# An encoder layer in one launch: the second embedding sum moved behind the fourth tile, and another order for the last two products and the final norm

## Chip, cores and metric

The kernel runs on one core of a Trainium2 chip. The metric is the device time of one execution in microseconds (us). Six kinds of queue matter below: TensorE (PE in the profile, with its weight loads as PEld), VectorE (DVE), ScalarE (ACT), GpSimd (POOL), SyncE (SP, which here only issues loads and stores), and the DMA engines that all these transfers share.

## The reference

One layer of a bidirectional encoder over a sequence of 1024 tokens of width 1024, all in float32. The parts before the first norm (retention, windowed attention, output projection) are not touched by the change. What follows is this:

```python
h = _layer_norm(ALPHA * h + mix, ln1_gain[i], ln1_bias[i])
g = h @ w_ffn_gate[i]
up = h @ w_ffn_up[i]                                # hidden width 2816
ffn = (jax.nn.silu(g) * up) @ w_ffn_down[i]
ple = p[i] @ w_ple_proj[i]                          # p: 1024 x 256
ple_gate = jax.nn.sigmoid(h @ w_ple_gate[i])        # 1024 x 1024 weight
h = _layer_norm(ALPHA * h + ffn + ple_gate * ple, ln2_gain[i], ln2_bias[i])
```

`_layer_norm(x, g, b)` is `(x - mean) * rsqrt(var + 1e-5) * g + b` over the 1024 columns of a row.

## The kernel before, in words

**Arithmetic.** Every float32 operand of a large product is split in two: a high part, copied by ScalarE (L71), and the low part that is left, subtracted by VectorE (L72). A product of 128x128 by 128x512 is then three matmuls (high by high, high by low, low by high; `mm3` at L77 to L79, `mm3c` at L763 to L765). The large matrix products are not made in four quadrant products of a 2x2 block scheme with eight terms but by a seven-product scheme (Strassen's kind): sums and differences of blocks are multiplied, and each of the products 1 to 7 is added to or subtracted from one or more quadrants of the result. Outputs of 128x512 are accumulated in eight PSUM banks, in four pairs with the tags `mm`, `s`, `t`, `o`.

**Stages.** Retention and attention run until about 370 us, the output projection and the first norm until about 470 us, then the gate of the per-layer embedding, the gate and up projections (about 555 to 870 us), the down projection, and the second norm.

**Order.** Inside a manual scope the order of the instructions on an engine is the order of the program; outside it a scheduler chooses the order from its own estimates. One scope holds TensorE and SyncE from early on. A second scope, `es3`, holds VectorE, ScalarE and GpSimd until `es3.close()`, which stands in the embedding stage. The whole down projection is in a scope that holds all five engines. SyncE's loads and stores go out in the order of its queue, each waiting for its data; GpSimd issues the accumulating DMAs, which add a tile in memory to one that is already in place.

**The embedding stage** (from about 470 us). `t_sums` (L995 to L1038) gives a list of steps that make the left operands of products 5, 6, 7 and 4, called sums 1 to 4, from blocks of the normed h: `both` takes three VectorE passes for a sum, `less` takes two (L1011, L1012; the third sum's are at L1004 to L1006), each over 128x1024, and `put` splits it (L71, L72). A sum has two halves, q = 0 and 1. Ahead of product 5 stand four tiles that finish a quadrant: for each, TensorE makes 12 matmuls into a bank, then `first_tile` calls `embed` (L1051 to L1062): four to six matmuls for p @ W_pe into another bank, the sigmoid on ScalarE, the product of both on VectorE (L1059, which frees that bank), and an addition into the tile's accumulator (L1060). Steps of the second sum are put between these tiles in VectorE's order: the half 0 of the second sum behind the second and third tile, half 1 and half 0 of the third sum ahead of product 5, the rest of the third sum inside product 5, the fourth sum inside product 6. Each of the products 5, 6, 7 and 4 is 48 matmuls into four banks; its results are added to others on VectorE (L1072 and `add4`).

**The down projection.** The 2816 hidden columns are cut in eleven pairs of blocks, and these in two segments of five and six (`SEG`). A unit is one product of one block pair: `dload` brings the blocks (and, for some, an accumulating DMA on GpSimd's queue makes their sum, L1340), `dprep` splits them, `dmm` does the matmuls (four row tiles, three matmuls each), and after a product's last unit `dpost` adds the four banks to the accumulators `acc`. There are 77 units; `d_step` does one and loads and splits ahead. The last two products are number 7 of the second segment (72 matmuls), which is subtracted from the right halves of tiles 0 to 3 (L1398), and number 4 (72 matmuls), which is added to the left halves (L1396, with the row sums; tile 3's at L1398). Tiles 4 to 7 are complete some time before that, since product 3 finishes them.

**The second norm.** For tiles 4 to 7 (`ln2_steps`) it is: squares with their sum on ScalarE (L1413), two scalar steps on VectorE and two on GpSimd (L1408 to L1449), one scaling pass on ScalarE over 1024 columns (L1452), one multiplication by the gain on VectorE, and an accumulating DMA that adds the bias (L1456). The list `later` spreads these steps over the units of the last products, and their stores (L1512) go out on SyncE ahead of those of tiles 0 to 3. For tiles 0 to 3 (`tail`) it is four VectorE passes over 512 columns: two for the mean and the gain (`center`, L1434), two for the deviation and the bias (`scale`, L1440), with no DMA but the stores; tile 3, `LAST`, takes its statistics by BATCH_NORM_STATS2 on VectorE (L1400).

Of the kernel before, what the change touches and what calls it, by code (L numbers as in the profile page):

```python
# [12 lines left out]
ALU = mybir.AluOpType  # L13
# [29 lines left out]
def layer(tc, xT, xn, w_first, w_mt, w_rv, w_out, w_pg, w_pe, pT, w_gu, w_dn,  # L43
# [951 lines left out]
    def t_sums():  # L995
# [21 lines left out]
        def step(n, q, parts=(0, 1)):  # L1017
# [19 lines left out]
            [lambda k=k: step(2, 0, (k,)) for k in range(2)] + \  # L1037
            [lambda n=n, q=q: step(n, q) for n, q in ((2, 1), (3, 0), (3, 1), (4, 0), (4, 1))]  # L1038
# [61 lines left out]
    for k in range(4):  # L1100
# [19 lines left out]
    product(6, Y, True, TT[2], steps[7:9])  # L1120
# [250 lines left out]
    def dmm(p, n, k, ts, first, stop):  # L1371

        a, b = dops[p, n]
        for t in ts:
            c = slice(t * P, (t + 1) * P)
            mm3c(dbank[k][t], a[:, 0, c], a[:, 1, c], b[:, 0, :], b[:, 1, :], first, stop)

    hs = [slice(h * HF, (h + 1) * HF) for h in range(2)]
    accd, R, later = [], [], []
# [12 lines left out]
    def addto(t, h, b, op=ALU.add, done=False):  # L1392
# [6 lines left out]
        if done and t == LAST:  # L1399
            dve.bn_stats(stts[t][:, 6 * h:6 * h + 6], half(t, h))  # L1400
        elif done:
            act.activation(ct([P, HF], "sg", 2), half(t, h), AF.Copy, accum_out=stts[t][:, h:h + 1])

    LAST = 3

# [9 lines left out]
    def var(t):  # L1415

        stt = stts[t]
        if t == LAST:
            dve.bn_aggr(stt[:, 12:14], stt[:, 0:12])
            dve.tensor_scalar(stt[:, 12:13], stt[:, 12:13], -1.0, None, ALU.mult)  # L1420
        else:
            negmean(t)
            squares(t)

    def rstd(t):
        stt = stts[t]
        if t != LAST:
            dve.tensor_scalar(stt[:, 13:14], stt[:, 2:3], stt[:, 3:4], 1.0 / D, ALU.add, ALU.mult)
# [3 lines left out]
    def center(t):  # L1432
        for h in range(2):
            x = half(t, h)  # L1434
            dve.scalar_tensor_tensor(x, x, stts[t][:, 12:13], ln2[0][:, hs[h]], ALU.add, ALU.mult)

    def scale(t):
        for h in range(2):
            x = half(t, h)
            dve.scalar_tensor_tensor(x, x, stts[t][:, 15:16], ln2[1][:, hs[h]], ALU.mult, ALU.add)  # L1440
            sp.dma_start(out[t][:, hs[h]], x)

    def ln2_steps(t):
# [7 lines left out]
        def second():  # L1451
            act.activation(x, x, AF.Identity, bias=stt[:, 11:12], scale=stt[:, 15:16])  # L1452

        def third():
            dve.tensor_tensor(x, x, ln2[0], ALU.mult)
            pool.dma_start(x, ln2[1], accum_op=ALU.add)  # L1456
# [249 lines left out]
```

## Time and profile before

| | |
|---|---|
| median of three runs | 1199.84 us (1199.11 to 1200.37) |
| the profiled execution | 1199.99 us |
| its span (first to last instruction) | 1198.0 us |
| granted TensorE clock, mean | 0.998 of full speed |
| last matmul begins | 1188.70 us |
| last store issued | 1195.04 us |

All times in the views are counted from the span's start. A row of the timeline gives start, duration, engine, line, operation, tiles written and read, shape, and how many of them; in brackets the wait ahead of it and what ended it. A row of the waits gives the engine, the operation that waited, what released it, then the total, the count and the longest. A row of the windows gives the stretch, its length, the busy time with the number of instructions of TensorE, its weight loads, VectorE, ScalarE and GpSimd, then SyncE's, the granted clock, the mean busy share of the DMA engines and what they moved in GB/s.

### The profile page before, as it was taken

How to read it: one execution, taken by the hardware profiler on the slowest of the kernel's cores; microseconds unless marked ns; L12 is line 12 of the kernel's file. 1: busy time of each engine (PE TensorE's matmuls, PEld its weight loads, DVE VectorE, ACT ScalarE, POOL GpSimd, SP SyncE). 2: the span in 40 equal slices, each digit the busy share in tenths (PEclk: the TensorE clock that was granted, in tenths of full speed). 3: DMA queues.
4: the chain of work that ended last, by engine and by line, in shares of the span. 5: the costliest groups of instructions: out<-in, count | busy, mean ns of one | idle time of the engine just before them, and what ended most of it. 6: DMA issues, size and time to landing. Idle time of an engine off the chain costs nothing.

```text
span 1198.0 us, 16664 instructions
## 1 busy us (share of the span) xinstructions
PE 1181.0 (99%) x5892; PEld 983.9 (82%) x5892; DVE 771.5 (64%) x1346; ACT 542.5 (45%) x1046; POOL 363.8 (30%) x342
## 2 busy tenths in 40 slices
PE   9999999999999999999999999999999999999996
PEld 7888888888888888788888888888888888888885
DVE  5654788877767788947744555545554565775668
ACT  5566238676786257203323332333322325562463
POOL 2001020202010022002756465555746342034232
PEclk9999999999999999999999999999999999999999
DMA  6335635434336864666233311332123169999977
GB/s 251 110 136 211 250 120 212 160 123 162 121 126 232 324 232 167 237 219 211 88 123 132 130 64 71 132 132 98 78 88 132 71 202 300 355 276 207 263 182 210
DMA packets 78098, 207.80 MB, mean 173 GB/s; under 512 B 9024, under 2 KB 13248, under 8 KB 78016
## 3 DMA queue, kind: packets, MB, share of 16 engines
q1 hardware_dynamic: 69376, 189.98, 44.0%
q0 software_dynamic: 8640, 16.78, 8.0%
q8 instruction: 46, 0.75, 0.2%
q14 instruction: 36, 0.29, 0.1%
HBM read 139.35 MB, written 62.13 MB: 168 GB/s over the span
## 4 chain that ended last, share of the span: by engine, by line
PE 94%; DVE 3%; ACT 1%; issue 1%; DMA 0%; POOL 0%; DVEq 0%; SPq 0%; ACTq 0%
PE bmm L77 6%; PE bt L763 6%; PE bt L764 6%; PE bt L765 6%; PE bmm L79 6%; PE bmm L78 6%; PE bs L763 6%; PE bs L764 6%; PE bs L765 6%; PE bo L763 5%; PE bo L764 5%; PE bo L765 5%; PE bmm L764 5%; PE bmm L763 5%; PE bmm L765 5%; PE bo L553 2%
## 5 line engine op out<-in xcount | busy, mean ns | idle before, releaser
L77 PE MATMUL bmm<-H,w 128*128 128x512 f32 x240 | 96.8, 403 | 0.4 <-ACT H L71 0.4
L79 PE MATMUL bmm<-H,w 128*128 128x512 f32 x240 | 94.1, 392 | 0.0
L78 PE MATMUL bmm<-H,w 128*128 128x512 f32 x240 | 93.8, 391 | 0.0
L1168 POOL TENSOR_TENSOR H<-ln 128x512 f32<-128x512 f32 x22 | 29.2, 1327 | 180.9 <-DMA ln<-in_w_gu 174.3
L1198 POOL TENSOR_TENSOR ev<-ev 128x512 f32<-128x512 f32 x33 | 54.9, 1664 | 91.2 <-DVE ev L1213 64.2
L72 DVE TENSOR_TENSOR w<-H,w 128x512 fp32r<-128x512 f32 x44 | 39.1, 889 | 63.1 <-ACT w L71 63.1
L72 DVE TENSOR_TENSOR w<-raw,w 128x512 fp32r<-128x512 f32 x56 | 45.3, 810 | 45.7 <-ACT w L71 45.2
L514 POOL COPY sc<-skb 128x1 f32<-128x1 f32 x64 | 13.0, 208 | 188.3 <-PE bt L541 149.4
L1196 ACT ACTIVATE ev<-ev 128x512 f32<-128x512 f32 x33 | 20.9, 632 | 103.5 <-DVE ev L1213 103.5
L1202 POOL TENSOR_TENSOR ev<-ev,ev 128x512 f32<-128x512 f32 x44 | 62.7, 1436 | 2.6
L72 DVE TENSOR_TENSOR u<-H,u 128x512 fp32r<-128x512 f32 x47 | 37.1, 790 | 38.9 <-ACT u L71 38.6
L77 PEld LDWEIGHTS bmm<-H,w 128*128 128x128 f32 x240 | 45.2, 188 | 10.5 <-ACT H L71 1.3
L79 PEld LDWEIGHTS bmm<-H,w 128*128 128x128 f32 x240 | 45.0, 188 | 10.0
L78 PEld LDWEIGHTS bmm<-H,w 128*128 128x128 f32 x240 | 45.1, 188 | 7.7
L71 ACT ACTIVATE u<-H 128x512 fp32r<-128x512 f32 x47 | 29.7, 631 | 43.5 <-PE bt L765 9.0
L523 ACT ACTIVATE sc<-sc,st 128x385 f32<-128x385 f32 (+1 forms) x64 | 37.2, 584 | 25.3 <-DVE st L521 25.2
L519 DVE CUSTOM_DVE_ANT_0 sc<-cst,bs,skb 128x384 f32<-128x384 f32 (+1 forms) x64 | 34.9, 576 | 16.3 <-PE bs L518 15.7
L71 ACT ACTIVATE w<-raw 128x512 fp32r<-128x512 f32 x56 | 34.7, 624 | 17.1 <-PE bo L79 7.0
L475 POOL TENSOR_TENSOR sm<-sm,cst 128x8 f32<-128x8 f32 x8 | 15.6, 1950 | 86.9 <-DVE sm L474 86.9
L874 POOL TENSOR_TENSOR stt<-stt,cst 128x1 f32<-128x1 f32 x8 | 12.1, 1514 | 91.2 <-DVE stt L873 91.2
L1172 POOL TENSOR_TENSOR H<-raw,H 128x512 f32<-128x512 f32 x22 | 37.8, 1718 | 0.0
L71 ACT ACTIVATE w<-H 128x512 fp32r<-128x512 f32 x44 | 27.4, 622 | 21.4 <-PE bs L765 6.3
(802 smaller groups left out, 3822.6 us busy)
## 6 DMA issues: line engine op xcount, KB each, us to landing
ad<-ev SPq DMA_DIRECT2D x33, 512.0 KB, 2.7
pgd<-pro SPq DMA_DIRECT2D x28, 512.0 KB, 2.8
raw<-in_w_gu SPq DMA_DIRECT2D x22, 512.0 KB, 4.3
ln<-in_w_gu SPq DMA_DIRECT2D x22, 512.0 KB, 3.5
raw<-ad SPq DMA_DIRECT2D x40, 256.0 KB, 5.5
ln<-ad SPq DMA_DIRECT2D x37, 256.0 KB, 6.7
H<-in_w_dn SPq DMA_DIRECT2D x33, 256.0 KB, 7.7
wod<-aq SPq DMA_DIRECT2D x15, 512.0 KB, 2.6
```

Of the source, the lines that this page charges most:

```text
L71: act.activation(hi, raw, AF.Copy)
L72: dve.tensor_tensor(lo, raw, hi.bitcast(F32), ALU.subtract)
L77: pe.matmul(o, lh, rh, start=start, stop=False)
L78: pe.matmul(o, lh, rl, start=False, stop=False)
L79: recent[0] = pe.matmul(o, ll, rh, start=False, stop=stop).ins.name
L523: act.activation(sc[g][:, :nk + 1], sc[g][:, :nk + 1], AF.Exp, bias=st_[:, 1, j, g:g + 1], accum_out=st_[:, 2, j, g:g + 1])
L763: pe.matmul(o, lh, rh, start=start, stop=False, skip_group_check=True)
L764: pe.matmul(o, lh, rl, start=False, stop=False, skip_group_check=True)
L765: pe.matmul(o, ll, rh, start=False, stop=stop, skip_group_check=True)
L1172: pool.tensor_tensor(s[3], a(0, 1), s[0], ALU.subtract)
L1198: pool.tensor_tensor(c[:, 1, :], c[:, 0, :], c[:, 1, :], ALU.mult)
L1202: pool.tensor_tensor(self.ev[dst][:, 0, :], left, right, op)
```

## The change

In the embedding stage, the second sum is no longer made between the four tiles: both of its halves stand behind the fourth tile, ahead of product 5. `es3.close()`, the end of the scope that holds VectorE, ScalarE and GpSimd to the program's order, moves from before product 5 to behind it.

At the end, of product 7's units for tiles 2 and 3 only the first two are done at its place; the other four, with the subtraction, are done between the tiles of product 4 (`rest`), which for these two tiles is then summed in a fresh bank, and the held bank is also added to the left half. Tiles 0 and 1 are as they were, and product 4 adds to their banks. The last tile is made in two halves of 256 columns, each with its own statistics, into a scratch tile `lst`. Tiles 0 to 2 are normed as tiles 4 to 7 are: one pass on ScalarE, one multiplication on VectorE, and an accumulating DMA for the bias (tile 2 in two halves of 512 columns). The steps of the norm of tiles 4 to 7 are spread further: fewer of them stand beside product 7, more between the tiles of product 4. SyncE's stores come in the order 4, 5, 6, 7, 0, 1, the first half of 2, the first half of 3, the second half of 2, and two quarters of 3.

```diff
@@ t_sums
         return [lambda k=k: [step(1, q, (k,)) for q in range(2)] for k in range(2)] + \
-            [lambda k=k: step(2, 0, (k,)) for k in range(2)] + \
-            [lambda n=n, q=q: step(n, q) for n, q in ((2, 1), (3, 0), (3, 1), (4, 0), (4, 1))]
+            [lambda n=n, q=q: step(n, q) for n in (2, 3, 4) for q in range(2)]
@@ the four tiles
-        if k in (1, 2):
-            steps[k]()
+        if k == 1:
+            steps[1]()
     gate_w(5, (2, 3))
     first_tile(3)
-    es3.close()
-    for k in range(3, 5):
+    for k in range(2, 4):
         steps[k]()
     gate_w(6)
     Z = four("b")
-    product(5, Z, True, TT[1], steps[5:7], True)
+    product(5, Z, True, TT[1], steps[4:6], True)
+    es3.close()
...
-    product(6, Y, True, TT[2], steps[7:9])
+    product(6, Y, True, TT[2], steps[6:8])
@@ tail
-    def tail(products):
...
+    def tail(k, grp):
+        held, whole = dbank[k], (0, 1)
+        def products(t, cols=slice(0, HF)):
+            for q in grp:
+                dmm(4, q, k, [t], t not in whole and q == grp[0], q == grp[-1], cols)
+        def rest(t):
+            for q in grp[2:]:
+                dmm(7, q, k, [t], False, q == grp[-1])
+            b = held[t]
+            held[t] = bank("o")
+            return b
+        def total(t):
+            addto(t, 0, held[t], done=True)
+            negmean(t)
+        def store(t, pieces=(slice(0, D),)):
+            for c in pieces:
+                sp.dma_start(out[t][:, c], accd[t][:, c])
+        steps = {t: ln2_steps(t, hs if t == 2 else (slice(0, D),)) for t in range(LAST)}
+        f, m, w = ({t: x[i] for t, x in [*steps.items(), *split4.items()]} for i in range(3))
+        w[5](); f[6](); squares(7)
+        products(0)
+        total(0); squares(0); m[6](); f[7](); w[6]()
+        products(1)
+        f[0](); m[7](); total(1); squares(1); w[7]()
+        store(4); store(5)
+        m[0](); f[1](); m[1]()
+        b = rest(2)
+        addto(2, 1, b, ALU.subtract, done=True)
+        dve.tensor_tensor(half(2, 0), half(2, 0), b, ALU.add)
+        w[0](); w[1]()
+        products(2)
+        total(2); squares(2); f[2]()
+        store(6); store(7)
+        b = rest(LAST)
+        addto(LAST, 1, b, ALU.subtract)
+        m[2]()
+        dve.bn_stats(lst[:, 0:6], half(LAST, 1))
+        w[2]()
+        dve.tensor_tensor(half(LAST, 0), half(LAST, 0), b, ALU.add)
+        store(0); store(1)
+        for n in range(2):
+            c = slice(n * 2 * P, (n + 1) * 2 * P)
+            x = accd[LAST][:, c]
+            if n:
+                held[LAST] = bank("mm")
+            products(LAST, c)
+            dve.tensor_tensor(x, x, held[LAST][:, c], ALU.add)
+            dve.bn_stats(lst[:, 6 + 6 * n:12 + 6 * n], x)
+        dve.bn_aggr(lst[:, 18:20], lst[:, 0:18])
+        dve.tensor_scalar(lst[:, 20:21], lst[:, 19:20], EPS, None, ALU.add)
+        pool.tensor_tensor(lst[:, 21:22], lst[:, 20:21], cst[:, C_MH:C_MH + 1], ALU.pow)
+        store(2, hs[:1])
+        for h in range(2):
+            x = half(LAST, h)
+            dve.scalar_tensor_tensor(x, x, lst[:, 18:19], ln2[0][:, hs[h]], ALU.subtract, ALU.mult)
+        for c in (hs[0], slice(HF, HF + 2 * P), slice(HF + 2 * P, D)):
+            x = accd[LAST][:, c]
+            dve.scalar_tensor_tensor(x, x, lst[:, 21:22], ln2[1][:, c], ALU.mult, ALU.add)
+            sp.dma_start(out[LAST][:, c], x)
+            if c == hs[0]:
+                store(2, hs[1:])
@@ ln2_steps(t, pieces): the pass on ScalarE, and the multiplication with its accumulating DMA, once for each piece
@@ dpost, behind product 3 of the second segment
-                later.extend([[], [q[1], f[0]], [m[0], q[2], f[1]], [w[0], m[1], q[3], f[2]], [w[1], m[2], f[3]], [m[3]],
-                              [w[2], w[3]]])
-                later[-1].extend(lambda u=u: sp.dma_start(out[u], accd[u]) for u in range(4, NT))
+                later.extend([[f[4]], [m[4]], [lambda: squares(5)], [lambda: squares(6)], [], [], [f[5], m[5], w[4]]])
@@ d_units, mm and post
-            if (p, s) == seq[-2]:
-                if n == grp[-1]:
-                    for t in range(4):
-                        for q in grp[-2:]:
-                            dmm(p, q, k, [t], False, q == n)
-                elif n != grp[-2]:
-                    dmm(p, n, k, range(4), False, False)
+            if (p, s) == seq[-2] and n == grp[-1]:
+                for t in range(2):
+                    for q in grp[-2:]:
+                        dmm(p, q, k, [t], False, q == n)
+            elif (p, s) == seq[-2]:
+                if n != grp[-2]:
+                    dmm(p, n, k, range(2), False, False)
+                if n in grp[:2]:
+                    dmm(p, n, k, range(2, 4), False, False)
...
-                for t in range(4):
+                for t in range(2 if (p, s) == seq[-2] else 4):
                     dpost(p, s, t)
```

Several statements that stand on lines of their own in the file are put on one line here, with semicolons.

More of the change, by code (lines that the diff above doesn't have):

```diff
@@ L1413, in squares, with ln2_steps @@
             act.activation(ct([P, HF], "sg", 2), half(t, h), AF.Square, bias=stt[:, 12:13], accum_out=stt[:, 2 + h:3 + h])
[L1415 to L1423, printed above, removed]
     def rstd(t):
         stt = stts[t]
-        if t != LAST:
-            dve.tensor_scalar(stt[:, 13:14], stt[:, 2:3], stt[:, 3:4], 1.0 / D, ALU.add, ALU.mult)
+        dve.tensor_scalar(stt[:, 13:14], stt[:, 2:3], stt[:, 3:4], 1.0 / D, ALU.add, ALU.mult)
         dve.tensor_scalar(stt[:, 14:15], stt[:, 13:14], EPS, None, ALU.add)
         pool.tensor_tensor(stt[:, 15:16], stt[:, 14:15], cst[:, C_MH:C_MH + 1], ALU.pow)
[L1432 to L1443, printed above, removed]
+    def ln2_steps(t, pieces=(slice(0, D),)):
         x, stt = accd[t], stts[t]
```

70 lines of the change are left out of this document (40 added, 30 removed).

## The prediction

> **What bounds the kernel now.** I read the page's busy table first, then what TensorE (PE) waited for, then the timeline at the two places the change touches.
>
> ```profile
> PE 1181.0 (99%) x5892; PEld 983.9 (82%) x5892; DVE 771.5 (64%) x1346; ACT 542.5 (45%) x1046; POOL 363.8 (30%) x342
> ```
> ```profile
> PE bmm L763 <- DVE sg L1059: 1.8, 1, 1.8
> ...
> PE bo L763 <- DVE sg L1059: 0.7, 1, 0.7
> PE bs L763 <- DVE acc L1398: 0.6, 1, 0.6
> ```
>
> TensorE is busy 99% of the span. There is little to win: the two waits on L1059 (the embedding), the one on L1398 (the start of the last product), and what lies behind the last matmul. The profiled execution took 1199.99 us, 1.99 beyond its span of 1198.0 and 0.15 above the median of 1199.84; I add to 1199.99. About 0.2%, 2.4 us, can be told from no change.
>
> **The embedding.** The timeline of TensorE, VectorE (DVE) and ScalarE (ACT):
>
> ```profile
> 485.49 0.39 PE L79 MATMUL bo<-u,p 128*128 128x512 f32 x1
> 485.71 0.39 PE L763 MATMUL bmm<-w,H 128*128 128x512 f32 x1
> 499.61 0.39 PE L763 MATMUL bt<-w,H 128*128 128x512 f32 x1
> 510.49 0.39 PE L763 MATMUL bt<-w,H 128*128 128x512 f32 x1
> ...
> 481.85 0.68 DVE L1059 TENSOR_TENSOR sg<-sg,bo 128x512 f32<-128x512 f32 x1
> 482.44 1.22 DVE L1011 TENSOR_TENSOR ln<-h,ln 128x1024 f32<-128x1024 f32 x1
> 487.59 0.68 DVE L1059 TENSOR_TENSOR sg<-sg,bmm 128x512 f32<-128x512 f32 x1
> 489.92 0.68 DVE L1059 TENSOR_TENSOR sg<-sg,bo 128x512 f32<-128x512 f32 x1
> 494.53 2.35 DVE L1006 TENSOR_TENSOR H<-H,h 128x1024 f32<-128x1024 f32 x2
> 500.21 2.35 DVE L72 TENSOR_TENSOR H<-H,H 128x1024 fp32r<-128x1024 f32 x2
> 504.75 0.67 DVE L1072 TENSOR_TENSOR H<-raw,bt 128x512 f32<-128x512 f32 x1
> ...
> 486.56 2.19 ACT L71 ACTIVATE H<-ln 128x1024 fp32r<-128x1024 f32 x2 [1.61 <-DVE ln L1012]
> ```
>
> Product 6 (499.61 to 510.49) is 48 matmuls in 10.88 us, 0.2267 each. Product 5, as many, needs 13.90 (485.71 to 499.61): it loses 3.0 us, because its second and fourth banks are still read by L1059, which stands behind L1011 and L1012 of the second sum. In the changed order of VectorE that sum comes behind the fourth tile. The third tile's L1059 then follows its matmuls at 484.6 and the fourth's at 485.9 (485.49 + 0.39), both before TensorE needs the banks. Product 5 ends at 496.6: **-3.0 us**.
>
> What is late next is the third sum, operand of product 7. A 128x1024 pass costs VectorE 1.14 (two in 2.35), a 128x512 one 0.60. Today the third sum is split from 500.21 to 502.5, and product 7 wants it at 510.49: 8 us of cover. In the compiled order of the changed kernel, the second sum starts behind the fourth tile, at 487.2 (485.9 and two passes over 512 columns). From there until the third sum's last pass VectorE has 16 passes of 1.14 (18.2 us): four of the second sum (L1011, L1012) and its two low parts (L72), the four of the *fourth* sum, put in between, five of the third sum's own six and its first low part. To these come four additions of product 6 (L1072, 2.4 us) and 1.5 us of waits, most of it for ScalarE's half of the second sum's first split (2.19 for two). The third sum's last pass starts at 487.2 + 18.2 + 2.4 + 1.5 = 509.3 and ends at 510.5; ScalarE's high part ends at 511.6, the low part at 512.9. Product 7 now starts at 507.5 (496.6 + 10.88) and needs the second half of that operand from its seventh matmul, 508.9, and its low part with the ninth, 509.3. That matmul goes at 513.0 rather than 509.3: **+3.7**. In the kernel before it goes at 510.49 + 8 x 0.2267 = 512.3. The place comes out **0.7 us later**, not 3.0 earlier. The second sum itself is in time by some tenths (low part at 497.9, wanted at 498.2). From there TensorE waits for nothing until 1172, so 0.7 is carried through.
>
> **The end: TensorE.**
>
> ```profile
> 1155.39 0.39 PE L763 MATMUL bs<-u,u 128*128 128x512 f32 x1
> 1172.51 0.47 PE L763 MATMUL bs<-H 128*128 128x512 f32 x1 [0.64 <-DVE acc L1398]
> 1188.70 0.39 PE L765 MATMUL bmm<-u,u 128*128 128x512 f32 x1
> ...
> 1161.37 0.21 DVE L1408 TENSOR_SCALAR stt<-stt 128x1 f32<-128x1 f32 x1
> 1168.19 0.69 DVE L72 TENSOR_TENSOR u<-h,u 128x512 fp32r<-128x512 f32 x1
> 1171.68 1.28 DVE L1398 TENSOR_TENSOR acc<-acc,bs 128x512 f32<-128x512 f32 x2
> ...
> 1160.49 0.62 ACT L71 ACTIVATE h<-raw 128x512 fp32r<-128x512 f32 x1
> 1164.37 1.24 ACT L1452 ACTIVATE acc<-acc,stt 128x1024 f32<-128x1024 f32 x1 [0.28 <-POOL stt L1449]
> 1165.52 0.71 ACT L1413 ACTIVATE sg<-acc,stt 128x512 f32<-128x512 f32 x1
> ...
> 1163.18 0.56 POOL L1430 TENSOR_TENSOR stt<-stt,cst 128x1 f32<-128x1 f32 x1 [5.30 <-DVE stt L1429]
> 1163.82 0.52 POOL L1449 TENSOR_TENSOR stt<-stt 128x1 f32<-128x1 f32 x1
> ...
> 54.48 0.28 PE L517 MATMUL bs<-k,aq 128*128 128x256 f32 x1
> 54.83 0.28 PE L518 MATMUL bs<-kz,aq 128*128 128x256 f32 x1
> ```
>
> Product 7 ends today after 72 matmuls at 1171.7; the first matmul of product 4 goes at 1172.51, 0.8 lost to L1398. With 24 of them deferred, TensorE is there after 48, at 1166.3. But the addition that it waits for stands behind the low part of the last operand unit (L72 at 1168.19), and ScalarE's high part before that now stands behind tile 4's normalising pass, moved ahead of two operand units. Its inputs: VectorE's two scalar steps from 1161.5, GpSimd's 0.56 + 0.52, so ScalarE waits from 1161.5 to 1163.2, then 1.14 for the pass, 1.04 for two L71, 1.42 for tile 5's squares, 1.04 for two L71: last low part at 1168.0, addition at 1168.6 to 1169.3, product 4 at 1169.4. Lost: 3.1 against 0.8. The last tile in halves costs little: four 256-column matmuls stand 0.118 apart (54.48 to 54.83), so 36 x 0.118 against 18 x 0.2267 is +0.17. The last matmul is **2.5 us later**, 1191.4.
>
> **The end: VectorE and ScalarE.** Tiles 0 to 2 give up four 512-column passes each on VectorE for one 1024-column multiply there, one pass on ScalarE and an accumulating DMA; two additions more (lines 1485 and 1499 of the changed kernel) for the deferred banks. The order now chains the engines: tile 0's squares before tile 6's pass on ScalarE, that before tile 6's multiply on VectorE. Worked through with the rows' durations, the accumulating DMAs are issued at 1171.4, 1173.7, 1178.8, 1181.1 (tiles 4 to 7), 1184.3, 1185.4 (0, 1), 1190.5 and 1191.2 (halves of 2). VectorE is late when the last half lands (1191.6): it finishes tile 2's multiply and tile 3's second addition first and ends its last pass at 1196.4.
>
> ```profile
> 1189.85 0.69 DVE L1400 BATCH_NORM_STATS2 stt<-acc 128x6 f32<-128x512 f32 x1
> 1193.60 1.41 DVE L1440 SCALAR_TENSOR_TENSOR acc<-acc,stt,u 128x512 f32<-128x512 f32 x2
> ```
>
> Today that is 1195.0 (1193.60 + 1.41): **+1.4** by the engines alone.
>
> **The end: DMA.** The view of the DMA queues from 1172 to 1191, the stretch itself, and the 1-us slices from 1160:
>
> ```profile
> q0 software_dynamic: 576, 2.10, 58.0%
> q1 hardware_dynamic: 1137, 3.14, 42.8%
> ...
> 1172.00:1191.00 19.00, 16.58 (x72) 13.44 (x72) 17.10 (x38) 8.89 (x20) 5.44 (x10) 1.00 1.01 276
> ...
> GB/s 162 43 6 0 0 8 0 0 0 0 0 0 197 197 180 209 197 291 344 213 229 262 279 250 229 328 295 397 373 389 379 6 170 354 0 301 223 0 0 8
> ...
> 1170.67 0.91 POOL L1456 DMA_DIRECT2D acc<-u  x1 [4.56 <-ACT sg L1413]
> SPq L1512 <- DMA acc<-u: 38.5, 4, 28.8
> ```
>
> The DMA engines are full for these 19 us (share 1.01). Four accumulates (2.10 MB on q0) take 58% of it: 2.76 us each. Six outputs' worth of stores (3.14 MB) take 42.8%: 1.36 each. The change adds three accumulates, 8.3 us of a full resource, and issues five of seven later than the last is issued today. Tile 6's, issued at 1178.8, moves data from 1180.2 (1.35 behind the issue, as 1170.67 to the slice at 1172). From there five accumulates and seven stores remain: 5 x 2.76 + 7 x 1.36 = 23.3 us, so the last data pass at 1203.5; today the last full slice is 1196 to 1197. SyncE issues stores in order, each behind its tile's accumulate, so even tile 3's last pieces stand behind tile 2's second half. Of the two ends the later sets the time: **+6.7**, against 1.4.
>
> The Trainium skill, "DMA: Bandwidth & Descriptors", section "Anatomy of one DMA", fits a GpSimd-issued DMA as 2.0 us fixed plus its bytes over 436 GB/s, and so gives an estimate of 1.2 us of data for 512 KB. By that the queue would be free early and VectorE's +1.4 would be the end. The trace disagrees: 2.76 us an accumulate.
>
> **Sum.** 1199.99 + 0.7 + 6.7 = 1207.4; I say 1207.0, since the stores may overlap a little better.
>
> **Rivals.**
> - *The queue keeps up* (accumulates cost less when fewer stores run beside them): only VectorE's chain counts, 1199.99 + 0.7 + 1.4 = 1202.1. Against it: share 1.01. Chance 0.14, half of it within the bound.
> - *The third sum is in time* (its last pass ends before 507.5, 3 us earlier than I work out): -3.0 whole, 1199.99 - 3.0 + 6.7 = 1203.7. Chance 0.12. With the rival before, 1198.4: no change that can be told, 0.05.
> - *Faster, as a free VectorE gives it.* If VectorE is idle when the last half lands, the last addition, its statistics (estimates 0.41 each, from 0.69 for 512 columns), 0.4 of scalar steps, two passes of 0.67 and 1.5 for the scaled pieces make 4.1, where today 5.9 pass from 1189.1 to 1195.0. With the 0.8 at L1398 and the 3.0 gone, +0.17 for the halves: 1194.6. It decides at tile 2's multiply, which must be over by 1190, and the accumulates must have landed. Chance 0.15.
> - *The clock.* Both stalls, of 2.9 and 3.1 us, could slow TensorE behind them. At the end it was granted full speed until 1193.36, 4.3 us after the last matmul ended:
>
> ```profile
> 1193.00:1193.50 0.50, 0.00 (x0) 0.00 (x0) 0.50 (x2) 0.00 (x0) 0.00 (x0) 0.86 1.00 369
> ```
>
>   (0.86 over half a microsecond, then 0.5.) Half speed for 4.3 us would cost 2.1: 1209.5. Chance 0.08. The Trainium skill, "TensorE: Matmul & The Clock Gate", "The HAM clock gate", halves the clock after an idle window of about 3.4 us; both stalls stay below that, the trace's 4.3 bears it out.
>
> **How the numbers follow.** Forecast 0.46. Faster by over 0.2%: 0.15. Within: 0.05 + 0.07 = 0.12. Slower: 0.73. The range 1200.0 to 1210.0 leaves out the faster rival and 1198.4, and takes in the clock.
>
> **What would show it.** TensorE's waits on L1059 of 1.8 and 0.7 gone, and one of about 3 us in product 7 on L71 or L72 of H; at product 4's start a wait near 2.9 in place of 0.6; full DMA slices until some 5 us behind VectorE's last pass, and SyncE waiting for accumulates at the end. No wait in product 7 makes the first part wrong, idle DMA slices after 1185 the second.

## The result, and the profile after

The changed kernel took 1208.03 us (median of six executions, 1206.72 to 1212.02), the kernel before, beside it, 1200.22. The ratio is 1.0068, with a 95% interval of 1.0050 to 1.0087: slower, by 8 us. A second set of five executions gave 1209.20 against 1199.79, ratio 1.0077 (1.0063 to 1.0091). The forecast was 1207.0.

There are two profiles of it. The first is of the execution of 1212.02 us (span 1210.2), 4 us above the median; the second of one of 1206.38 (span 1204.4), the fastest of its five. So the two stand near the two ends of the changed kernel's spread. Where TensorE waited longest, in the first:

```profile
PE bs L763 <- ACT sg L1411: 4.6, 1, 4.6
PE bt L763 <- ACT H L71: 2.7, 1, 2.7
```

and in the second:

```profile
PE bt L763 <- ACT H L71: 2.7, 1, 2.7
...
PE bs L763 <- ACT sg L1411: 0.5, 1, 0.5
```

The two waits on L1059 are gone, and one of 2.7 us on L71 of H, the operand of product 7, is there in both. The wait at product 4's start was 4.6 in one and 0.5 in the other. Lines after about L1037 have moved by one or more against before: L1058 is what L1059 was, L1071 what L1072 was, L1397 and L1395 what L1398 and L1396 were. (The third sum's three passes are L1005 to L1007, in both kernels.)

The embedding stage in the timeline of the first profile:

```profile
493.49 1.22 DVE L1011 TENSOR_TENSOR ln<-h0b,ln 128x1024 f32<-128x1024 f32 x1
...
501.52 1.22 DVE L1012 TENSOR_TENSOR ln<-ln,h0b 128x1024 f32<-128x1024 f32 x1
...
509.62 1.22 DVE L1007 TENSOR_TENSOR H<-H,h 128x1024 f32<-128x1024 f32 x1
511.95 1.23 DVE L72 TENSOR_TENSOR H<-H,H 128x1024 fp32r<-128x1024 f32 x1 [1.12 <-ACT H L71]
510.86 1.06 ACT L71 ACTIVATE H<-H 128x1024 fp32r<-128x1024 f32 x1 [5.89 <-DVE H L1007]
511.97 0.63 PE L763 MATMUL bt<-w,H 128*128 128x512 f32 x1 [2.69 <-ACT H L71]
513.23 0.79 PE L765 MATMUL bt<-w,H 128*128 128x512 f32 x1 [0.20 <-DVE H L72]
```

The rows that read h0b are the fourth sum's (four of them, first and last shown): they are mixed in with the second sum's last passes and the third sum's first, and all four end before the third sum's second half begins at 506.15. The third sum's last pass (L1007) runs from 509.6 to 510.8, and product 7 waits for its two parts. The windows around this wait and around the one at product 4, first profile (the column behind GpSimd's busy time is the granted clock):

```profile
511.00:512.00 1.00, 0.03 (x1) 0.03 (x1) 0.05 (x1) 1.00 (x2) 0.00 (x0) 1.00 0.75 307
513.00:515.00 2.00, 1.80 (x5) 1.48 (x5) 2.00 (x3) 0.81 (x1) 0.00 (x0) 0.50 0.28 113
516.00:517.00 1.00, 1.00 (x6) 0.79 (x5) 0.73 (x2) 0.00 (x0) 0.00 (x0) 1.00 0.00 0
1169.00:1170.00 1.00, 0.00 (x0) 0.00 (x0) 1.00 (x2) 1.00 (x3) 0.00 (x0) 1.00 0.00 0
1171.00:1177.00 6.00, 3.60 (x9) 2.86 (x10) 3.90 (x7) 4.58 (x11) 2.19 (x3) 0.50 0.00 0
```

Each of the two waits was followed by half clock: by the trace's clock for 3.41 us from 512.19, and for 6.83 us from 1170.96, which is still inside the second wait.

The end, in the second profile: GpSimd's accumulates (first, third and last two), the DMA queues from 1170 to 1204, windows, and VectorE's last passes.

```profile
1171.39 0.91 POOL L1434 DMA_DIRECT2D acc<-u  x1 [0.49 <-issue]
...
1179.02 0.89 POOL L1434 DMA_DIRECT2D acc<-u  x1 [2.67 <-DVE stt L1416]
...
1193.17 1.78 POOL L1434 DMA_DIRECT2D acc<-u  x2 [1.98 <-DVE acc L1433]
```
```profile
q0 software_dynamic: 1152, 3.67, 57.9%
q1 hardware_dynamic: 1584, 4.20, 32.5%
```
```profile
1180.00:1190.00 10.00, 10.00 (x61) 8.95 (x60) 5.78 (x11) 6.02 (x12) 6.04 (x7) 1.00 1.03 247
1190.00:1202.00 12.00, 0.56 (x5) 0.36 (x3) 8.28 (x18) 1.52 (x2) 3.52 (x5) 0.68 1.02 282
1202.00:1204.00 2.00, 0.00 (x0) 0.00 (x0) 0.00 (x0) 0.00 (x0) 0.00 (x0) 0.50 0.46 155
```
```profile
1197.53 1.54 DVE L1519 SCALAR_TENSOR_TENSOR acc<-acc,p,u 128x512 f32<-128x512 f32 x3
```

VectorE is done at 1199.1, but the DMA engines are full (share 1.02) until 1202: seven accumulates take 57.9% of 34 us, 2.81 us each, and eight outputs of stores 32.5%, 1.38 each.

### The profile page after: what moved, and what is told of

The parts are those of the page before. It is cut to its first block, busy times and chain, and to the rows that moved or that the text cites. A ratio compares the mean times of both kernels' runs of the same rounds, so it can differ in the third digit from the quotient of the medians.

```text
span 1210.2 us, 16712 instructions
## 1 busy us (share of the span) xinstructions
PE 1185.4 (98%) x5910; PEld 988.2 (82%) x5910; DVE 770.8 (64%) x1342; ACT 546.5 (45%) x1050; POOL 370.9 (31%) x349
## 4 chain that ended last, share of the span: by engine, by line
PE 78%; DMA 8%; issue 5%; DVE 5%; ACT 2%; POOL 2%; SPq 0%; DVEq 0%; POOLq 0%; ACTq 0%
PE bmm L77 6%; PE bmm L79 6%; PE bmm L78 6%; PE bs L763 4%; PE bs L765 4%; PE bs L764 4%; PE bt L765 4%; PE bt L763 4%; PE bt L764 4%; PE bmm L765 3%; PE bmm L763 3%; PE bmm L764 3%; PE bo L765 3%; PE bo L763 3%; PE bo L764 3%
## 5 line engine op out<-in xcount | busy, mean ns | idle before, releaser
L71 ACT ACTIVATE u<-H 128x512 fp32r<-128x512 f32 x47 | 29.6, 631 | 45.2 <-PE bt L765 9.0
L523 ACT ACTIVATE sc<-sc,st 128x385 f32<-128x385 f32 (+1 forms) x64 | 37.2, 584 | 25.4 <-DVE st L521 25.3
L71 ACT ACTIVATE w<-raw 128x512 fp32r<-128x512 f32 x56 | 34.8, 624 | 17.9 <-PE bo L79 7.7
L71 ACT ACTIVATE w<-H 128x512 fp32r<-128x512 f32 x44 | 27.3, 622 | 21.4 <-PE bs L765 6.3
```

Source lines behind the costliest of these rows:

```text
L71: act.activation(hi, raw, AF.Copy)
L523: act.activation(sc[g][:, :nk + 1], sc[g][:, :nk + 1], AF.Exp, bias=st_[:, 1, j, g:g + 1], accum_out=st_[:, 2, j, g:g + 1])
```

## The experiments

All times are medians; the ratio is to the kernel before on the same chip.

| run | us | before | ratio (95%) |
|---|---|---|---|
| embed_only | 1202.23 | 1200.16 | 1.0016 (1.0005 to 1.0028) |
| embed_fix | 1198.32 | 1200.16 | 0.9981 (0.9970 to 0.9993) |
| end_only | 1207.83 | 1200.16 | 1.0065 (1.0040 to 1.0090) |
| end_no_accum | 1206.58 | 1200.16 | 1.0046 (1.0031 to 1.0062) |
| end_m4_late | 1205.92 | 1200.33 | 1.0042 (1.0029 to 1.0055) |
| defer_only | 1207.25 | 1200.33 | 1.0058 (1.0044 to 1.0073) |
| end_no_issue | 1203.55 | 1200.33 | 1.0027 (1.0014 to 1.0040) |
| both_off | 1202.85 | 1199.76 | 1.0022 (1.0012 to 1.0032) |
| after_fix | 1203.62 | 1199.76 | 1.0035 (1.0023 to 1.0048) |
| best_b | 1199.67 | 1200.33 | 0.9992 (0.9984 to 1.0001) |
| best_c | 1197.05 | 1199.76 | 0.9979 (0.9970 to 0.9989) |
| after_again | 1209.20 | 1199.79 | 1.0077 (1.0063 to 1.0091) |

### The embedding: embed_only and embed_fix

embed_only is the kernel before with the first four edits of the diff (the steps of the sums and `es3.close()`).

> Only the embedding part of the change; the end as before. Theory A (the second sum is made in time, but the fourth sum's passes stand ahead of the third's on VectorE, and product 7 waits; in the profile of the changed kernel the wait was 2.7 us and the granted clock 0.5 for 3.4 us behind it): product 5 gains 3.0, product 7 loses 3.7 and 1.7 more at half clock, so +2.4 us, about 1202.6, or +0.7 (1200.9) in executions where the clock isn't lowered. Theory B (the place is free, because the units behind it have slack that takes up any delay): 1200.2, no difference.

It was 2.07 us slower than before, near the 2.4 of theory A. Its profile has the wait of 2.7 us on L71 of H and the clock at half speed for 3.41 us behind it:

```profile
PE bt L763 <- ACT H L71: 2.7, 1, 2.7
```

Its twelve executions run from 1200.67 to 1205.50, and only one has a trace, so how many of them had the half clock is not known. Theory B is out: the delay is carried to the end.

embed_fix keeps VectorE's and ScalarE's order by hand until behind product 7, and puts the fourth sum there (against embed_only):

```diff
-    product(5, Z, True, TT[1], steps[4:6], True)
-    es3.close()
+    product(5, Z, True, TT[1], steps[4:5], True)
...
-    product(6, Y, True, TT[2], steps[6:8])
-    add4(u2, s1, Y)
-    product(7, Y, False, TT[3])
-    add4(c22, s1, Y)
+    def plus(out_, k, then=None):
+        dve.tensor_tensor(out_[k], s1[k], Y[k], ALU.add)
+        if then is not None:
+            steps[then]()
...
+    product(6, Y, True, TT[2], [lambda k=k: plus(u2, k, {1: 5, 3: 6}.get(k)) for k in range(4)])
+    product(7, Y, False, TT[3], [lambda k=k: plus(c22, k, {2: 8, 3: 9}.get(k)) for k in range(4)])
     add4(c22, c22, Z)
+    es3.close()
```

(Cut at each `...`, and between the products. Step 4 is the third sum's first half; steps 5 and 6 are its second half and the fourth sum's first; 8 and 9 the two stages of the fourth's second half.)

> The embedding part alone, but with VectorE's and ScalarE's order kept by hand until product 7 is done: second sum, third sum, two of product 6's additions between its halves, and only then the fourth sum, inside product 7. The work is the same. Theory A (the order of the fourth sum against the third is the whole loss): no wait in product 5 nor in product 7, -3.0 us against before, 1197.2. Theory B (VectorE has too much to do between 487 and 510 us in any order): the wait stays above 2 us in product 6 or 7, or moves to product 4, and the time is 1200 or more.

The same work in another order is faster than before, 0.9981 (0.9970 to 0.9993), and 3.9 us under embed_only. The order of the fourth sum against the third was the loss. Its waits:

```profile
PE bs L763 <- DVE acc L1402: 1.8, 1, 1.8
...
PE bt L765 <- DVE H L72: 0.5, 1, 0.5
```

The gain was 1.8 us, not 3.0. In the profiled execution 0.5 is lost in product 7, and the wait at product 4's start, 0.6 before, is 1.8: TensorE comes there earlier, the additions that it needs do not.

### The end: four kernels in a square

end_only is the kernel before with the rest of the diff.

> Only the end part of the change; the embedding as before. Theory A (accumulates and the stall at product 4's start are there without the embedding's delay): the change's +7.8 us less the embedding's 2.4, +5.4, 1205.6, with a wait of 3 to 4.6 us at product 4's start and the DMA engines full until the end. Theory B (the embedding's delay is what set the end's chain off): under +2, below 1202.

The end part alone costs 7.7 us; theory B (below 1202) is out. Its six executions run from 1204.98 to 1214.13, and the interval of the ratio, 4.8 to 10.8 us, takes in the 5.4 that were expected. Part of this spread has nothing to do with the end: in its profile, of an execution of 1211.96, TensorE is 3.8 us later than in the kernel before as early as ahead of the embedding stage (3.5 in the profile of defer_only, below). So whether the two parts add up, 2.1 + 7.7 against 7.8 for the changed kernel, these runs can't tell.

end_no_accum leaves out the accumulates that the change adds:

```diff
-                pool.dma_start(x[:, c], ln2[1][:, c], accum_op=ALU.add)
+                if t > LAST:
+                    pool.dma_start(x[:, c], ln2[1][:, c], accum_op=ALU.add)
```

> The end part alone, without the bias of the second norm for tiles 0 to 2, that is without the four accumulating DMAs that the change adds (1.6 MB); tiles 4 to 7 keep theirs. Theory A (the full DMA queue sets the end): 7 or 8 us of transfers fall away, and VectorE's last pass with its store becomes the end, 2 to 4 us below the end part with them, about 1202.5, with the last store 3 us behind VectorE's last pass. Theory B (the stall at product 4 and VectorE's chain set the end, the DMAs only follow): within 1 us of the end part with them, about 1205.

The median fell by 1.25 us, less than the intervals can tell apart. Theory A's 1202.5 is missed by 4 us: without the added accumulates the end part is still 6.4 us slower than before. VectorE's chain is late without them: its last matmul, and VectorE's last passes:

```profile
1169.25 0.61 PE L763 MATMUL bs<-H 128*128 128x512 f32 x1 [3.00 <-ACT sg L1412]
...
1192.80 0.28 PE L765 MATMUL bt<-u,u 128*128 128x256 f32 x1
...
1199.06 1.54 DVE L1521 SCALAR_TENSOR_TENSOR acc<-acc,p,u 128x512 f32<-128x512 f32 x3
```

Product 4 starts at 1169.25, after a wait of 3.0 us, and the clock is at half speed for the 3.41 us that follow. VectorE ends at 1200.6, 7.8 us behind the start of the last matmul (6.3 before). So the span of 1204.3, 6.4 more than before, is explained without the added accumulates: 2.4 more of wait and 1.7 of clock make the last matmul 4.1 later than before, 1.5 more the chain behind it, 0.8 more the store.

end_m4_late moves tile 4's normalising pass out of ScalarE's way, with the accumulates left in:

```diff
-                later.extend([[f[4]], [m[4]], [lambda: squares(5)], [lambda: squares(6)], [], [], [f[5], m[5], w[4]]])
+                later.extend([[f[4]], [], [lambda: squares(5)], [lambda: squares(6)], [], [], [m[4], f[5], m[5], w[4]]])
```

> The end part alone, with tile 4's normalising pass on ScalarE moved back behind the last operand units (it stood ahead of two of them, and waited 1.6 us for GpSimd there). Theory A (this pass holds the last operands, and with them the additions that product 4 waits for): ScalarE is 2.8 us earlier with the last unit, the wait at product 4's start falls from 3.0 or 3.2 to under 1 us, the clock stays at 1.00, and the time falls by 3 to 4 us against the end part as it is, to about 1204. Theory B (the deferred units alone make TensorE early, and what it waits for is where it was): the wait stays above 2 us and the time within 1 us of the end part's 1207.8.

The stall is gone, as in theory A: no wait at product 4 is left in the profile, the clock is 1.00 there, and the last matmul starts at 1188.6. But the median fell by only 1.9 us, which is within end_only's spread. What sets the end is now something else:

```profile
1195.51 1.54 DVE L1520 SCALAR_TENSOR_TENSOR acc<-acc,p,u 128x512 f32<-128x512 f32 x3
```
```profile
1190.00:1197.00 7.00, 0.00 (x0) 0.00 (x0) 6.70 (x14) 0.72 (x2) 2.78 (x3) 0.76 1.05 271
1197.00:1202.00 5.00, 0.00 (x0) 0.00 (x0) 0.05 (x1) 0.00 (x0) 0.00 (x0) 0.50 1.03 343
```

VectorE ends at 1197.05, and for 5 us more the DMA engines alone work, at a share of 1.03; the span is 1203.8. both_off takes both away, that pass and the accumulates of tiles 0 to 2:

> The end part alone with both suspects out: tile 4's normalising pass behind the last operand units, and no bias (no accumulating DMA) for tiles 0 to 2. Each alone took 1.3 to 1.9 us off 1207.8. Theory A (the DMA queue and the chain behind TensorE are two ends of nearly equal length, so that each hides what the other would give): together 5 to 6 us less, 1202, with VectorE's last pass at about 1197 and the last store 3.7 us behind. Theory B (the two costs are parts of one sum): 1.9 + 1.3 less, 1204.6.

1202.85, 5.0 under end_only. The square, in us:

| | accumulates of tiles 0 to 2 there | left out |
|---|---|---|
| tile 4's pass ahead of the operand units | 1207.83 | 1206.58 |
| tile 4's pass behind them | 1205.92 | 1202.85 |

The lower right is clear of both its neighbours, by 3.7 and 3.1 us. The upper left is known only to some 3 us, so the medians alone do not show that the two gains hide each other; the profiles do. With product 4's stall and no added accumulates the span ends 3.7 us behind VectorE's last pass (1200.6 to 1204.3): that is the last store. With both there, in end_only, it ends 4.9 behind (1204.6 to 1209.5), and with the accumulates alone, in end_m4_late, 6.8. So there are two ends, VectorE's chain with its store and the DMA queue; where product 4 stalls the queue's is only 1.2 us the later, and where it doesn't, 3.1. The windows of both_off show the second gone:

```profile
1190.00:1192.00 2.00, 0.00 (x0) 0.00 (x0) 1.85 (x4) 0.00 (x0) 0.00 (x0) 1.00 0.69 262
1192.00:1196.00 4.00, 0.00 (x0) 0.00 (x0) 3.90 (x10) 0.00 (x0) 0.99 (x1) 0.72 0.00 0
```

The DMA engines are idle from 1192 to 1196, and VectorE's end (1196.3) with its store makes the span of 1200.1.

### Where the stall comes from: defer_only

The kernel before with nothing but product 7's last four units of tiles 2 and 3 done between product 4's tiles:

```diff
         for t in range(4):
-            products(t)
+            if t > 1:
+                for q in grp[2:]:
+                    dmm(7, q, k, [t], False, q == grp[-1])
+                b, bs[t] = bs[t], bank("o")
+                addto(t, 1, b, ALU.subtract, done=True)
+                dve.tensor_tensor(half(t, 0), half(t, 0), b, ALU.add)
+            for q in grp:
+                dmm(4, q, k, [t], t > 1 and q == grp[0], q == grp[-1])
...
```

(Cut: the rest of the edit leaves these units out at product 7's place, as the change does.)

> The kernel before with one thing of the change: product 7's last four units for tiles 2 and 3 are done between the tiles of product 4. Norms, spreading, whole last tile and stores as before. Theory A (deferral takes 24 matmuls, 5.4 us, out from in front of the wait, so TensorE stands earlier before the same additions): the wait at product 4's start grows from 0.6 to 2.5 or 3 us, the last matmul is 2 to 2.5 us later, the time 1202.5, and 1204 where the clock drops. Theory B (the wait in the changed kernel comes from the moved norm steps alone): no wait over 1 us, 1200.5.

```profile
PE bs L763 <- DVE acc L1398: 4.7, 1, 4.7
```

The deferral alone makes a wait of 4.7 us and costs 6.9 us (1.0044 to 1.0073), both well above theory A's 2.5 to 3 us and 1202.5 to 1204. There are 24 matmuls, 5.4 us, fewer in front of the wait, and the additions that TensorE needs come no earlier: they start 14.7 us behind the issue of the last accumulating load, as they do in the kernel before. Here they stand behind two gain multiplications of 1.22 us on VectorE (L1455), in the changed kernel behind tile 4's pass on ScalarE. With the deferral and neither of these (end_m4_late) there is no wait, and with the multiplications and no deferral (before) one of 0.6. So it takes both: units taken out from in front of the wait, and norm steps ahead of what is waited for. Tile 4's early pass without the deferral was not run.

### GpSimd's part in the chain: end_no_issue

The end part without any accumulate of the norm (the `pool.dma_start` of `ln2_steps` deleted; tiles 4 to 7 too get no bias).

> The end part alone without any accumulating DMA of the second norm: tiles 0 to 2 and 4 to 7 get no bias. Against the run that leaves out those of tiles 0 to 2 alone (1206.6). Theory A (GpSimd is a step of the chain at the end: behind an issue its power operation takes 1.47 to 1.94 us where it takes 0.55 alone, and ScalarE's pass and VectorE's multiplication wait for it): 2 us less, about 1204.5, power operations of 0.55 and VectorE's last pass 2 us earlier. Theory B (GpSimd's part is hidden, TensorE's stall and VectorE's order set the end): 1206.6, within 0.7.

3.0 us under end_no_accum. GpSimd's power operations for tiles 6, 0 and 1, first there, then in end_no_accum:

```profile
1175.52 0.55 POOL L1418 TENSOR_TENSOR stt<-stt,cst 128x1 f32<-128x1 f32 x1 [2.93 <-DVE stt L1417]
...
1182.60 0.55 POOL L1418 TENSOR_TENSOR stt<-stt,cst 128x1 f32<-128x1 f32 x1 [3.19 <-DVE stt L1417]
...
1185.50 0.55 POOL L1418 TENSOR_TENSOR stt<-stt,cst 128x1 f32<-128x1 f32 x1 [2.08 <-DVE stt L1417]
```
```profile
1175.33 0.89 POOL L1418 TENSOR_TENSOR stt<-stt,cst 128x1 f32<-128x1 f32 x1
...
1181.20 1.65 POOL L1418 TENSOR_TENSOR stt<-stt,cst 128x1 f32<-128x1 f32 x1
...
1184.16 1.93 POOL L1418 TENSOR_TENSOR stt<-stt,cst 128x1 f32<-128x1 f32 x1
```

An issue takes GpSimd 0.9 us. It puts the power operation behind it off, into VectorE's next multiplication of 1.22 us, and beside that it takes 1.65 or 1.93 us. ScalarE's pass waits for it, and VectorE's next multiplication for that. What this is worth is read from VectorE's own chain, from tile 0's sum, the first thing there that waits for product 4, to the last pass. First without the issues, then in end_no_accum:

```profile
1177.24 0.69 DVE L1396 CUSTOM_DVE_ANT_0 acc<-acc,bs 128x512 f32<-128x512 f32 x1 [1.80 <-PE bs L765]
...
1199.06 1.54 DVE L1519 SCALAR_TENSOR_TENSOR acc<-acc,p,u 128x512 f32<-128x512 f32 x3
```
```profile
1175.21 0.69 DVE L1396 CUSTOM_DVE_ANT_0 acc<-acc,bs 128x512 f32<-128x512 f32 x1 [0.53 <-PE bs L765]
```

Both end at 1200.6, so the chain is 23.4 us long instead of 25.4. Nothing in it waits for TensorE behind that sum. The other 1.0 of the 3.0 is within the intervals; this kernel also moves fewer bytes, and that part was not tried apart.

### The change without its stalls, and two versions meant to be faster

after_fix is the whole change with embed_fix's order and end_m4_late's list.

> The whole change with its two stalls of TensorE taken out: the embedding's order kept by hand (fourth sum behind the third), and tile 4's normalising pass behind the last operand units. All seven accumulating DMAs are there. Theory A (the end is then the full DMA queue, which starts with the norms of tiles 4 to 7 and so comes earlier with the embedding's 2 to 3 us): 1203 to 1204, DMA engines full for some 25 us and 5 us or more from VectorE's last pass to the end. Theory B (without stalls the change is what it was meant to be, and VectorE's last pass sets the end): 1198 or less.

1203.62, within theory A: of the waits in product 7 and at product 4's start no more than 0.5 and 0.2 us is left, VectorE ends at 1195.0, and the span is 1201.8, 6.8 us longer. As in end_m4_late the DMA engines set the end (a share of 1.00 or more in every 2 us from 1172 to 1198, 0.99 to 1200).

best_b: embed_fix, with the gain multiplications of tiles 4 to 7 behind product 7's subtractions, the steps of each tile's norm directly behind its sum, and the last pass of tiles 0 to 2 on ScalarE and GpSimd (two lines of it):

```diff
+        act.activation(half(t, h), half(t, h), AF.Copy, scale=stts[t][:, 15:16])
+        pool.tensor_tensor(half(t, h), half(t, h), ln2[1][:, hs[h]], ALU.add)
```

> A version meant to be faster, with the order of the embedding kept by hand (second sum, third sum, fourth sum) and the end of the kernel before with two differences: the gain multiplications of tiles 4 to 7 all stand behind product 7's subtractions on VectorE (two stood ahead and made TensorE wait 1.8 us), and the second norm's last pass of tiles 0 to 2 is made by ScalarE (deviation) and GpSimd (bias) in place of VectorE. No deferral, no accumulate more. Theory A (VectorE's passes behind the last matmul are the end): 1.4 us less there and 1 to 1.8 us at product 4's start, so 1198.3 - 3 = 1195.3. Theory B (GpSimd's additions of 1.3 to 1.7 us for 512 columns come late instead, tile 2's second half last): 1197 to 1198.5.

A miss: 1199.67. The last matmul starts at 1186.0, 2.7 us earlier than before, but VectorE ends at 1195.0 as it did. Four multiplications in a row stand in front of tile 0's sum, each of tiles 0 to 2 has VectorE wait 1.7 us for ScalarE's squares, and beside GpSimd's additions VectorE's last two passes take 2.42 us instead of 1.41 (more on this below).

best_c: embed_fix, and only the gain multiplications of tiles 4 and 5 given to GpSimd:

```diff
-            dve.tensor_tensor(x, x, ln2[0], ALU.mult)
+            (pool if t < 6 else dve).tensor_tensor(x, x, ln2[0], ALU.mult)
...
-                later.extend([..., [w[0], m[1], q[3], f[2]], [w[1], m[2], f[3]], [m[3]], [w[2], w[3]]])
+                later.extend([..., [w[0], m[1], q[3], f[2]], [m[2], f[3]], [m[3]], [w[1], w[2], w[3]]])
```

> Meant to be faster than both: the embedding's order kept by hand, the end of the kernel before, and only the gain multiplications of tiles 4 and 5 (1.2 us each on VectorE, ahead of product 7's subtractions) given to GpSimd, which is idle there. Theory A (TensorE's 1.8 us at product 4's start goes, and VectorE has 2.4 us less to do before tile 0's sum): 1.5 to 2 us under the embedding's order alone (1198.3), 1196.5. Theory B (GpSimd's two passes slow VectorE beside them, or put off the powers of tiles 6 and 7 and with them the chain): 1198 to 1199.

1197.05 against 1199.76, ratio 0.9979 (0.9970 to 0.9989): faster than both kernels, and nearest to theory A. No wait at product 4 is left. Whether it beats embed_fix (0.9981) the intervals don't tell.

### The changed kernel once more: after_again

> The changed kernel once more, for a second profile: the first was of an execution 4 us above its median, with the granted clock at 0.5 for 6.83 us behind the wait of 4.64 us at product 4's start. Theory A (the clock is set by windows of 3.41 us that run on their own, and falls for one window more where a wait spans two of them): about 1207.5 to 1208.5 in the median; all falls of the clock in one execution lie whole multiples of 3.41 us apart; an execution near the median has a wait of about 3 us at product 4's start and 0.5 for 3.41 us behind it. Theory B (the wait of 4.64 us is the usual one): the profile shows it again at the median.

The median is 1209.20, above theory A's 1208.5. The second profile has a wait of 0.5 us at product 4 and no half clock there. So neither the 4.64 of the first nor theory A's 3 us is there in every execution; but as the second profile is of the fastest of five, it does not tell which wait is the usual one, and theory B stays open. The last accumulating load and the additions before product 4, first in the first profile, then in the second:

```profile
1160.90 0.86 POOL L1339 DMA_DIRECT2D h<-in_w_dn  x1 [1.13 <-DVE H L72]
1172.58 1.28 DVE L1397 TENSOR_TENSOR acc<-acc,bs 128x512 f32<-128x512 f32 x2
```
```profile
1155.81 0.86 POOL L1339 DMA_DIRECT2D h<-in_w_dn  x1 [0.54 <-DVE H L72]
1167.49 1.28 DVE L1397 TENSOR_TENSOR acc<-acc,bs 128x512 f32<-128x512 f32 x2
```

From the issue to the additions it is 11.68 us in both, and 11.68 too in end_only, end_no_accum and end_no_issue, the other three that have tile 4's pass ahead of the operand units. So this chain runs from the last load, while TensorE came to the wait at 1168.8 and 1167.8 (product 4's first matmul less its wait). How long it waits is how late that load is against TensorE; why the load is 5.1 us apart in two executions is not known.

That the clock's falls lie whole windows apart holds in the first profile, where there are three: (1170.96 - 512.19) / 3.413 = 193.0, (1201.68 - 512.19) / 3.413 = 202.0.

## Why the prediction was right, and where it was not

**Product 5's stall: right.** Both waits on L1059 are gone: from 480 to 500 us TensorE is busy for 20.00 us in the first profile, 17.56 before.

**The third sum: right, to half a microsecond.** Its last pass was to start at 509.3 and end at 510.5; it ran from 509.62 to 510.8. The ninth matmul of product 7 was to go at 513.0; it went at 513.23. Here the order of the passes, counted row by row, carried the number.

**What followed the stall: wrong.** I gave the clock 0.08 and wrote that both stalls stay below what lowers it. A wait of 2.69 us lowered it in all three profiles that have this wait (two of the changed kernel, one of embed_only), for 3.41 us, which costs 1.7: embed_only measured +2.07 where the step's sum says +0.7. The Trainium skill, "TensorE: Matmul & The Clock Gate", section "The HAM clock gate", describes free-running windows of about 3.4 us. The trace agrees on the windows: every fall is a whole number of 3.41 us from the others. It disagrees with my reading that a whole window must be idle: in the window that ended at 1170.96 TensorE still worked for 1.2 of 3.41 us. The 4.3 us at the end of the kernel before, which I took as bearing that reading out, show only where the windows' edges lay: that fall came at the end of the first window, 1189.95 to 1193.36, that lay wholly behind the last matmul.

**Product 4's start: right in the kernel it was worked out for.** 1169.4 was forecast without the embedding's delay, 1169.25 measured (end_no_accum). The wait there was to be 3.1, and was 3.0. But the step left out the half clock again (1.7 us), and that the last load varies by 5 us between executions, so that the wait is 0.5 in one and 4.6 in another. In the two profiles of the changed kernel the additions are 5.1 us apart and the spans 5.8; that the rest of its spread has the same cause was not shown.

**VectorE's chain: mis-sized.** I had the last pass end 5.0 us behind the last matmul's start (1191.4 to 1196.4; the step's own terms, 1188.70 + 2.5, give 1191.2). It is 7.8 in end_no_accum and in the first profile, 8.8 in the second. The term taken from before's rows, 0.56 us for GpSimd's power operation, is 1.65 and 1.93 here, beside VectorE's multiplications; without the issues that cause this the chain is 2.0 us shorter. So the "+1.4 by the engines alone" was +5.6: end_no_accum's VectorE ends at 1200.6, before's at 1195.0. Of the 4.2 between, 1.7 is the clock's.

**DMA: right in price, wrong in how far it stands alone.** 2.76 us an accumulate was forecast, 2.81 measured. Tile 4 to 6's were to be issued at 1171.4, 1173.7 and 1178.8; in the second profile the first is at 1171.39, the third at 1179.02, and the queue, which was to be full until 1203.5, was so until between 1202 and 1204. That agreement is luck: in the first profile the same issues are at 1176.48 and 1185.21. The queue is the last to end in both profiles, as forecast. But I put 5.3 us between its end and the one that VectorE sets. Counted from VectorE's last pass the span ends 4.9 and 5.3 us later, and 3.7 of that the store needs by itself (end_no_accum), so the queue is later by 1.2 and 1.6. Where nothing stalls (after_fix) it is later by 3.1. Without the added accumulates the end part is still 6.4 us slower than before. The price of the rival "the queue keeps up" (1202.1) falls for the same reason: without those transfers VectorE's chain alone gives 1206.58.

**The sum.** 1207.4 came out near 1208.03 in part by luck. The direction and the queue at the very end were forecast for reasons that hold. But the 6.7 was put down to the queue alone, and 6.4 of it is there without the queue's added load; the half clock and GpSimd's share in the chain, which make up 3.7 of these, were not in the sum for the end, and the embedding's term was 0.7 where 2.1 was measured. Why the parts, 2.1 and 7.7 as medians, come to no more than 7.8 together is within end_only's interval and not explained.

## What to carry to other kernels

Work taken out from in front of a wait is a gain only if what is waited for comes earlier too: price a deferral together with the queue of the engine that frees TensorE. When one cost is taken away and the time hardly moves, take the other away as well before calling the first one harmless; of two ends of nearly equal length each looks free alone. Where order on one engine is left to a scheduler, read the compiled order: here one order of the same passes cost 2.1 us and another gained 1.8.

## What the runs showed of the hardware

- A wait of TensorE need not fill a clock window. The falls of the clock cut a trace into windows of 3.413 us. Over all profiles, each window at full clock with TensorE idle for a share of 0.57 or more was followed by half clock (0.57, 0.64, 0.69, 0.76, 0.79, 0.84, 0.88 and more), and none with 0.52 or less was (the wait of 1.8 us on L1059 before lay in one of 0.51). In these profiles waits of up to 1.8 us cost their length, and a wait of 2.7 us cost 1.7 more. The length alone does not decide: a window's edge cut end_only's wait of 3.17 us into shares of 0.36 and 0.57.
- Coming back takes a window that is nearly full. At half clock, a window with TensorE idle for 0.20 (end_no_issue, from 1169.31) was followed by another at half clock, one with 0.09 (embed_only, from 512.88) by full clock.
- GpSimd and VectorE hold each other up. A VectorE pass over 512 columns with both inputs in SBUF took 1.43 us beside GpSimd's multiplication in best_c (0.68 to 0.69 alone), while the two subtractions that read a PSUM bank beside GpSimd's next one, the last two rows of VectorE here, took 0.68 and 0.69:

```profile
1165.19 1.43 DVE L72 TENSOR_TENSOR u<-ln,u 128x512 fp32r<-128x512 f32 x1 [2.38 <-ACT u L71]
...
1168.58 1.27 DVE L1402 TENSOR_TENSOR acc<-acc,bs 128x512 f32<-128x512 f32 x2
1169.77 0.68 DVE L1402 TENSOR_TENSOR acc<-acc,bmm 128x512 f32<-128x512 f32 x1
1171.00 0.69 DVE L1402 TENSOR_TENSOR acc<-acc,bmm 128x512 f32<-128x512 f32 x1 [0.55 <-PE bmm L765]
```
```profile
1163.67 2.40 POOL L1459 TENSOR_TENSOR acc<-acc,u 128x1024 f32<-128x1024 f32 x1
...
1169.52 2.41 POOL L1459 TENSOR_TENSOR acc<-acc,u 128x1024 f32<-128x1024 f32 x1
```

  The pass that began at 1165.19 ended at 1166.62, 0.55 behind GpSimd's end at 1166.07, so most of its own work fell behind that end. The Trainium skill, "SBUF — State Buffer", section "Summary: rules for kernel authors", says that of a VectorE operation with two SBUF inputs and a GpSimd operation that reads SBUF the second to issue is blocked until the first is done. The trace agrees for this pass. It shows GpSimd held up too, and there it was not the second: the power operation of 128x1 that took 1.93 us in end_no_accum began at 1184.16, 0.33 before VectorE's multiplication, and ended 0.38 behind it.
- What no run tells: the last tile's halves and the new order of stores were not tried alone.
